# Hybrid decoder trunk: decoding a scan block one step later, right in front of the encoding of the block two further on

## The chip, the core and the metric

The kernel runs on one core of a Trainium2 chip. The core has a matrix engine (TensorE, PE in the rows of the profile, with its weight loads listed apart as PEld), a vector engine (VectorE, DVE), a scalar engine (ScalarE, ACT), a general engine (GpSimd, POOL) and a queue engine that here only issues DMAs (SyncE, SP). The engines run side by side; each takes its own instructions in order and waits on semaphores for the others. The metric is the device time of one launch in microseconds.

## The reference, cut to what matters

A trunk of two layers for 256 positions of width 2048. Layer 0 is a Mamba-2 mixer beside block attention; the change doesn't touch it. Layer 1 is a diagonal complex state-space mixer (S5), and the change lies in its scan.

```
u, gate = split(x @ w_in)                     # 2048 -> 2 x 2048
u_g = u as 128 groups of 16 channels          # each drives 64 complex states
bu  = b_bar[g] @ u_g                          # encode into the states
h_t = lam_bar * h_{t-1} + bu_t                # scan over 256 positions
y   = real(c[g] @ h) + d * u                  # decode
y   = gelu(y)
ga, gb = split(y @ w_glu)
out = (ga * sigmoid(gb) * silu(gate)) @ w_out
x   = layer_norm(alpha * x + out)
```

## The kernel before, in words

**Weights.** All five weight matrices are streamed from memory as 432 chunks of 256 x 512 numbers, here called units. `split_to` loads a unit (SP, L222) and splits it into a high part (ACT, L225) and a low part (DVE, L227), because a product is built from three products of parts. It is called three units ahead of the unit that PE is at; four buffers hold units. PE multiplies a unit in `wmm` (L288, 24 rows of 128x256 in the profile's count) or in `xmm` (L271, 12 rows of 128x512).

**Jobs and steps.** All other work is emitted between the units by `pump`: first the jobs that must be done within the current product (`jobs`), then those that are spread evenly up to a goal (`back`). The scan of layer 1 is such a list. It is made of 16 blocks of 8 groups; `ssm(b)` enters the parts of block b under step numbers, with `at(t, f)`, and each step that is not empty becomes one entry of `back`. The entries are spread over 66 units, beginning at the second product of layer 1. With t = 2b the parts are:

- `load` at t-2: POOL issues the DMA of the block's tables (`wt`, four buffers, L1114)
- `table` at t-1: POOL writes the scan's factors (`rt`, L1121 and L1122)
- `enc` at t: 16 small matmuls on quarters of the array (64x64), from `wt` and the inputs `um` into the PSUM tile `enc` (one buffer, L1131; the profile counts 32 passes)
- `rec1` at t+1: DVE turns the states by their phases (L1141 to L1149)
- `rec2` at t+2: DVE scans and turns back (L1156 to L1159), result `gt` (two buffers)
- `dec` at t+3: 24 small matmuls of the same shape, from `um` (L1172) and `gt` (L1176), into the PSUM tile `dec` (one buffer; the profile counts 48 passes)
- `act` at t+4: ACT applies gelu from PSUM (L1182); after every second block POOL stores the result to memory (L1187, L1188)

After every fourth block the stored result is loaded back in another layout (`y_load`, POOL, L1201) and split into a high and a low part (`y_split`, ACT L1209 and DVE L1210). The product with `w_glu` reads these: `product_pair` runs twelve units on the results of the first twelve blocks and then four units on those of the last four.

**Order.** Within a step the parts stand in the order in which the blocks entered them. A build-time scheduler of the framework then sets the order of each engine's instructions from the order of emission, the dependences and its own estimate of times; it may put large matmuls between small ones. Semaphores come from the dependences. During the steps, jobs of the products stand on ACT too, among them the Silu of the gate half (L1225), which needs another function table than gelu.

Of the kernel before, what the change touches and what calls it, by code (L numbers as in the profile page):

```python
# [159 lines left out]
def trunk(tc, io, out):  # L160
# [8 lines left out]
    with ExitStack() as top:  # L169
# [23 lines left out]
        def big(tag, shape, dt=F32):  # L193
            return slot.tile(shape, dt, tag=tag, name=nm(tag))
# [877 lines left out]
        with ExitStack() as l1:  # L1072
# [3 lines left out]
            def w1(tag, shape, bufs=2, dt=F32):  # L1076
                return wk.tile(shape, dt, tag=tag, bufs=bufs, name=nm(tag))
# [13 lines left out]
            def u_load(hh):  # L1091
                j, h = hh // 2, hh % 2
                u = um[hh] = w1("um", [P, 12, 64], 3)
                for i in range(2):
                    src = ud[j][16 * h + 8 * i : 16 * h + 8 * i + 8].rearrange("q a c -> a q c")
                    at = 64 * (1 - i)
                    nc.gpsimd.dma_start(u[64 * i : 64 * i + 64, 0:8, :], src)
                    nc.gpsimd.dma_start(u[at : at + 64, 8:12, :], src[:, 1::2, :])
# [3 lines left out]
            def at(t, f):  # L1102
                steps.setdefault(t, []).append(f)
# [3 lines left out]
            def ssm(b):  # L1107
# [80 lines left out]
                            nc.gpsimd.dma_start(dst[1, :, 1 - i], ys[64:128, i])  # L1188

                t = 2 * b  # L1190
                at(t + 4, act)
                at(t + 3, dec)
                at(t + 2, rec2)
                at(t + 1, rec1)
                at(t, enc)
# [3 lines left out]
            def y_load(j):  # L1199
                y5[j] = w1("ut", [P, 4, S], 1)  # L1200
                nc.gpsimd.dma_start(y5[j], yd[j].rearrange("g a c -> (g a c)").rearrange("(f p t) -> p f t", p=P, t=S))  # L1201

            def y_split(j):
                if j == 0:
                    y5["h"] = big("A", [P, KT, S], F32R)
                    y5["l"] = big("B", [P, KT, S], F32R)
                yt = y5[j]
                fs = slice(4 * j, 4 * j + 4)
                A.activation(y5["h"][:, fs, :], yt, AF.Copy)  # L1209
                V.tensor_tensor(y5["l"][:, fs, :], yt, y5["h"][:, fs, :].bitcast(F32), op=OP.subtract)  # L1210

            for b in range(16):
                ssm(b)
                if b % 2 == 0:
                    at(2 * b - 2, lambda b=b: u_load(b // 2))
                if b % 4 == 3:
                    at(2 * b + 6, lambda b=b: y_load(b // 4))
                    at(2 * b + 9, lambda b=b: y_split(b // 4))
            sg1 = wk.tile([P, 2, D], F32, tag="sg1", bufs=1, name="sg1")
            for j in range(8):  # L1220
                ps = product("w" if j < 4 else "x", x1hl) if j else first1
# [105 lines left out]
```

## Time and profile before

| | us |
|---|---|
| median of 3 runs | 1364.88 |
| lowest, highest | 1363.3, 1366.78 |
| profiled execution | 1366.41 |
| its span, first to last instruction | 1364.6 |
| busy: PE / PEld / DVE / ACT / POOL | 1349.1 / 1214.1 / 982.8 / 673.3 / 372.3 |
| first encode to last decode | 915.5 to 1100.2 |

The times of the table's first three rows are of whole launches; the span is that of the instructions in the profiled one. In a row of the profile stand the engine, the line of the kernel, the operation, the tiles written and read, and the shape. PE's matmuls overlap in the array, so that the durations of rows in a sequence add up to more than the time they take; the time from one start to the next is what counts. "Idle before" is only a cost on an engine that bounds the stage.

### The profile page before, as it was taken

What the parts mean: (1) busy time and instruction counts of PE and PEld (TensorE: products, weight loads), DVE (VectorE), ACT (ScalarE), POOL (GpSimd) and SP (SyncE); (2) the same over time, 40 slices, a digit from 0 to 9 for tenths busy, and PEclk for the clock granted to TensorE, in tenths of its full rate; (3) what the DMA queues carried; (4) which work ended last, traced back from release to release, by engine and by line L of the source; (5) the groups of instructions that cost most, each with busy time, mean ns of one, the idle gap of its engine ahead of it and who ended that gap; (6) DMA issues with size and microseconds to landing.
All of it is one profiled execution on the core that took longest, in us unless ns stands there. A gap on an engine that the chain in (4) does not pass through costs nothing.

```text
span 1364.6 us, 25068 instructions
## 1 busy us (share of the span) xinstructions
PE 1349.1 (99%) x9918; PEld 1214.1 (89%) x9918; DVE 982.8 (72%) x1559; ACT 673.3 (49%) x869; POOL 372.3 (27%) x649
## 2 busy tenths in 40 slices
PE   9999999999999999999999999999999999999996
PEld 9999999998998998998988888899977788888885
DVE  5789746687688779689788766748788856555555
ACT  5565557764543543554554344344344545444441
POOL 0140000123027628616788700013243100000001
PEclk9999999999999999999999999899999999999998
DMA  8556555545546756756767779397888666666762
GB/s 308 173 156 201 176 169 166 155 140 170 184 125 208 254 164 205 261 169 207 256 203 229 216 231 315 121 303 247 288 269 300 210 211 191 187 189 187 256 215 78
DMA packets 80742, 283.02 MB, mean 207 GB/s; under 512 B 9840, under 2 KB 12528, under 8 KB 80112
## 3 DMA queue, kind: packets, MB, share of 16 engines
q1 hardware_dynamic: 68112, 239.33, 55.5%
q0 software_dynamic: 7328, 30.42, 6.8%
q10 hardware_dynamic: 5184, 11.67, 2.2%
q8 instruction: 78, 1.28, 0.4%
q14 instruction: 40, 0.33, 0.1%
HBM read 260.41 MB, written 20.97 MB: 206 GB/s over the span
## 4 chain that ended last, share of the span: by engine, by line
PE 94%; DVE 4%; DMA 1%; issue 1%; ACT 0%; POOL 0%; POOLq 0%; DVEq 0%
PE main L288 43%; PE main L271 43%; DVE wl L227 1%; PE aux L358 1%; PE enc L1131 1%; PE aux L794 1%; PE dec L1176 1%; PE aux L701 1%; PE aux L367 1%; DMA bc<-in_s5bc 1%; PE aux L906 1%; PE aux L874 1%; PE aux L764 0%; PE dec L1172 0%; PE aux L697 0%
## 5 line engine op out<-in xcount | busy, mean ns | idle before, releaser
L227 DVE TENSOR_TENSOR wl<-raw,wh 128x1024 fp32r<-128x1024 f32 x431 | 538.5, 1251 | 329.5 <-ACT wh L225 323.4
L225 ACT ACTIVATE wh<-raw 128x1024 fp32r<-128x1024 f32 x431 | 456.1, 1059 | 579.1 <-PE main L271 266.0
L288 PE MATMUL main<-A,wh 128*128 128x256 f32 x1408 | 402.6, 286 | 0.0
L288 PE MATMUL main<-B,wh 128*128 128x256 f32 x1408 | 400.1, 284 | 0.0
L288 PE MATMUL main<-A,wl 128*128 128x256 f32 x1408 | 399.9, 284 | 0.0
L288 PEld LDWEIGHTS main<-A,wh 128*128 128x128 f32 x1408 | 270.8, 192 | 0.6 <-issue 0.2
L288 PEld LDWEIGHTS main<-B,wh 128*128 128x128 f32 x1408 | 270.8, 192 | 0.4
L288 PEld LDWEIGHTS main<-A,wl 128*128 128x128 f32 x1408 | 270.7, 192 | 0.2 <-issue 0.2
L271 PE MATMUL main<-wl,A 128*128 128x512 f32 x512 | 200.4, 391 | 0.5 <-DVE wl L227 0.3
L271 PE MATMUL main<-wh,A 128*128 128x512 f32 x512 | 200.4, 392 | 0.0
L271 PE MATMUL main<-wh,B 128*128 128x512 f32 x512 | 200.0, 391 | 0.0
L271 PE MATMUL main<-wh,C 128*128 128x512 f32 x384 | 152.0, 397 | 0.0
L271 PE MATMUL main<-wh,F 128*128 128x512 f32 x384 | 150.0, 391 | 0.0
L271 PE MATMUL main<-wl,C 128*128 128x512 f32 x384 | 149.8, 390 | 0.0
L635 POOL TENSOR_TENSOR c<-c 128x8 f32<-128x8 f32 (+2 forms) x192 | 108.0, 581 | 28.8 <-DMA wb<-c 21.3
L271 PEld LDWEIGHTS main<-wl,A 128*128 128x128 f32 x512 | 96.2, 188 | 20.9 <-DVE wl L227 1.3
L271 PEld LDWEIGHTS main<-wh,B 128*128 128x128 f32 x512 | 96.2, 188 | 19.9
L271 PEld LDWEIGHTS main<-wh,A 128*128 128x128 f32 x512 | 96.2, 188 | 19.8 <-issue 0.2
L271 PEld LDWEIGHTS main<-wh,C 128*128 128x128 f32 x384 | 72.1, 188 | 15.5
L271 PEld LDWEIGHTS main<-wh,F 128*128 128x128 f32 x384 | 72.1, 188 | 15.4
L271 PEld LDWEIGHTS main<-wl,C 128*128 128x128 f32 x384 | 72.1, 188 | 14.3
L804 POOL TENSOR_TENSOR ssq<-ssq,c 128x256 f32<-128x256 f32 x16 | 17.6, 1099 | 210.2 <-ACT c L802 209.6
(279 smaller groups left out, 1680.6 us busy)
## 6 DMA issues: line engine op xcount, KB each, us to landing
raw<-in_wi SPq DMA_DIRECT2D x271, 512.0 KB, 4.0
raw<-in_wo SPq DMA_DIRECT2D x96, 512.0 KB, 4.3
raw<-in_wglu SPq DMA_DIRECT2D x64, 512.0 KB, 3.7
wt<-wb POOLq DMA_DIRECT2D x16, 896.0 KB, 7.6
wb<-ob ACTq DMA_DIRECT2D x16, 512.0 KB, 5.5
bc<-in_s5bc SPq DMA_DIRECT2D x16, 256.0 KB, 4.4
wb<-c POOLq DMA_DIRECT2D x16, 256.0 KB, 4.1
wb<-om ACTq DMA_DIRECT2D x16, 128.0 KB, 4.1
```

What stands on the lines that cost most here:

```text
L225: high = A.activation(wh, raw, AF.Copy)
L227: splits[n] = (high, V.tensor_tensor(wl, raw, wh.bitcast(F32), op=OP.subtract))
L271: T.matmul(ps[o], l[:, k, sl], r[:, j, :], start=start and i == 0, stop=stop and i == 2)
L288: T.matmul(pv[o // 2][:, o % 2, :], l[:, j, sl], r[:, k, :], start=first and i == 0 and o % 2 == 0, stop=end and i == 2 and o % 2 == 1, sk ...
L358: end = T.transpose(dst[:, i * P : i * P + P], s, ident)
L367: T.matmul(px[:64, 0:64], idle, idle, start=i == 0, stop=i == n - 1)
L635: G.tensor_tensor(p[:, :, :, 0:m], cs[:, :, :, 1 : m + 1], cs[:, i, :, n : n + 1].unsqueeze(1).to_broadcast([P, 2, 4, m]), op=OP.mult)
L701: T.matmul(pk[at : at + 64, a * 16 : a * 16 + 16], ev[:, a, 64 * i : 64 * i + 64], cv[:, a, i, :], start=True, stop=True)
L794: T.matmul(yo, xs[:, 0, xc], df[:, i, 0:256], start=True, stop=False)
L804: G.tensor_tensor(ssq, ssq, jk[:, f, :], op=OP.add)
L874: T.matmul(px[:, 128:384], qT[:, h, P:S], kT[:, h, :], start=True, stop=True)
L906: T.matmul(po, v[:, 0, hs], pT[:, i, 0:256], start=True, stop=False)
```

## The change

The decode of a block moves from step 2b+3 to step 2b+4, and gelu from 2b+4 to 2b+5. Step 2b+4 is the one in which block b+2 is encoded, and as block b entered its parts first, its decode stands directly in front of that encode. The load back and the split of the finished results move by one step as well. Nothing else is changed: no instruction is added or taken out.

```
                 t = 2 * b
-                at(t + 4, act)
-                at(t + 3, dec)
+                at(t + 5, act)
+                at(t + 4, dec)
                 at(t + 2, rec2)
                 at(t + 1, rec1)
                 at(t, enc)
...
                 if b % 4 == 3:
-                    at(2 * b + 6, lambda b=b: y_load(b // 4))
-                    at(2 * b + 9, lambda b=b: y_split(b // 4))
+                    at(2 * b + 7, lambda b=b: y_load(b // 4))
+                    at(2 * b + 10, lambda b=b: y_split(b // 4))
```

## The prediction

> **What bounds the kernel now.** I read the page first, then the list of waits of PE, then the sums of each engine over the scan stage, then PE's rows one by one.
>
> ```profile
> span 1364.6 us, 25068 instructions
> ...
> PE 94%; DVE 4%; DMA 1%; issue 1%; ACT 0%; POOL 0%; POOLq 0%; DVEq 0%
> ...
> PE aux L358 <- DVE D L1016: 1.4, 2, 1.3
> PE aux L367 <- POOL idle L362: 0.9, 1, 0.9
> PE main L288 <- DVE F L1030: 0.9, 1, 0.9
> PE main L288 <- ACT C L1026: 0.6, 2, 0.3
> PE main L271 <- DVE wl L227: 0.3, 1, 0.3
> ...
> 905.00:1101.00 196.00, 196.00 (x2248) 166.72 (x2247) 157.21 (x222) 89.32 (x101) 60.23 (x107) 1.00 0.81 259
> ```
>
> The chain that ends last is PE for 94% of the span. The five rows after it are all the waits of PE in the whole run, 4.1 us together, and no encode (L1131) or decode (L1172, L1176) is among them. The last row is the scan stage (columns: PE, PE weight loads, DVE, ACT, POOL, clock, DMA share, GB/s): PE is busy in all 196.0 us at the full clock, DVE in 157.2, ACT in 89.3, POOL in 60.2. So what PE does here is paid one for one, and what the other engines do is free as long as it isn't late.
>
> PE's rows around one whole decode and one whole encode (start, duration, instruction):
>
> ```profile
> 998.16 0.39 PE L271 MATMUL main<-wh,F 128*128 128x512 f32 x1
> 998.48 0.34 PE L1172 MATMUL dec<-um,wt 64*64 64x64 f32 x8
> 998.64 0.41 PE L1176 MATMUL dec<-gt,wt 64*64 64x63 f32 x16
> 998.87 0.30 PE L1172 MATMUL dec<-um,wt 64*64 64x64 f32 x8
> 998.99 0.41 PE L1176 MATMUL dec<-gt,wt 64*64 64x63 f32 x16
> 999.33 0.50 PE L271 MATMUL main<-wh,C 128*128 128x512 f32 x1
> 999.67 0.40 PE L271 MATMUL main<-wl,C 128*128 128x512 f32 x1
> 999.90 0.39 PE L271 MATMUL main<-wh,F 128*128 128x512 f32 x1
> ...
> 925.92 0.28 PE L288 MATMUL main<-C,wl 128*128 128x256 f32 x1
> 926.12 0.69 PE L1131 MATMUL enc<-um,wt 64*64 64x64 f32 x32
> 926.75 0.39 PE L288 MATMUL main<-C,wh 128*128 128x256 f32 x1
> 926.97 0.28 PE L288 MATMUL main<-F,wh 128*128 128x256 f32 x1
> 927.09 0.28 PE L288 MATMUL main<-C,wl 128*128 128x256 f32 x1
> ...
> 929.61 0.28 PE L288 MATMUL main<-C,wl 128*128 128x256 f32 x1
> 929.82 0.34 PE L1172 MATMUL dec<-um,wt 64*64 64x64 f32 x8
> 930.09 0.39 PE L288 MATMUL main<-C,wh 128*128 128x256 f32 x1
> 930.32 0.28 PE L288 MATMUL main<-F,wh 128*128 128x256 f32 x1
> ```
>
> Ends of matmuls are modelled, so I use starts. Undisturbed large matmuls start every 0.23 us (L271) or 0.12 us (L288). From 998.16 to 999.90 lie three large starts, 0.68 us by themselves, in 1.74 us: the decode of 48 passes costs 1.06. From 925.92 to 927.09 the same way: 1.17 - 0.36 = 0.81 for an encode of 32 passes. From 929.61 to 930.32: 0.71 - 0.24 = 0.47 for 8 passes, the first piece of a decode that stands in two pieces. A line through the three gives 0.015 us a pass, which the starts inside the decode confirm (998.87 to 998.99, 0.12 for 8), and a fixed price: 0.47 - 0.12 = 0.35, 0.81 - 0.48 = 0.33, 1.06 - 0.72 = 0.34. Each visit of PE to the 64x64 shape thus costs **0.34 us** whatever it does there. The rows show where: 998.16 to 998.48 is 0.09 longer than 0.23 on the way in; on the way out the first large matmul starts about 0.13 late and the second one (999.33 to 999.67) 0.11.
>
> **The change, part by part.**
>
> *Visits of PE.* In the built order of the kernel before, the 16 encodes make 17 visits (block 0's stands in two) and the 16 decodes 22 (those of blocks 0, 3, 7, 10, 13 and 15 stand in two, with large matmuls between): 39. In the built order of the changed kernel there are two for encode 0, one for encode 1, fourteen in which decode b-2 runs straight into encode b (b from 2 to 15), and decodes 14 and 15 alone, none of them in pieces: 19. Passes and large matmuls are the same in number. 20 visits fewer at 0.336 (the three fits, unrounded) are **-6.7 us**.
>
> *The seam.* No row of before shows a decode followed at once by an encode. Below, it costs nothing: the nearest row is the seam inside the decode, from L1172 to L1176 with other tiles and operands, where the next start comes after 0.12 us for eight passes as it does anywhere else (998.64 to 998.87, from L1176 back to L1172, is 0.23 for 16). Above, it costs a whole visit, 14 x 0.336 = 4.7 us. I take nothing, as the nearest row is of the same shape on the same engine. The Trainium skill (TensorEngine Tiling (Array Packing), Tiling Modes, key properties) states that a change of the tiling mode, and not one of the tile alone, drains TensorE; by it the seam is free as well, which no run here shows yet.
>
> *What the fixed price is.* Should the 0.09 on the way in be the first matmul's semaphore wait rather than the shape, each of the 14 seams keeps it: 14 x 0.09 = 1.3 us, and the sum is -5.4. The Trainium skill (TensorE: Matmul & The Clock Gate, Part 3, The cost: per-tile semaphore tail) speaks against the full gain: it gives a tail of 25 + 4.7 per tile + 26.3 ns per increment where packed tiles end, 70 ns for four tiles and one increment; as an estimate by that, the 14 merged visits keep 14 x 0.07 = 1.0 us and the sum would be -5.7, inside the bounds that the forecast has below without it. The trace speaks for the shape: the piece at 929.82, at whose end no other engine's work is released, pays the same 0.35.
>
> *Steps.* The stage has 40 non-empty steps where it had 39, spread over the same number of weight units: each comes 2.5% closer. Nothing on PE changes by that.
>
> *DVE.* The two reconstruction steps keep their places in the step list; a decode now has two steps instead of one between its input and itself. With 157.2 us of work in a stage that shrinks to 189, DVE is at 83% and hidden.
>
> *ACT, POOL and the DMAs.* Gelu (ACT, 16 x 0.38 us), the four stores after every second block (POOL, 0.62 each), the load back and the split of the result all move one step later, together. Two chains have to be looked at, and the buffers.
>
> ```profile
> 1005.23 1.05 ACT L225 ACTIVATE wh<-raw 128x1024 fp32r<-128x1024 f32 x1
> ...
> 1033.05 1.28 ACT L1225 ACT_TABLE_LOAD   x1
> 1034.35 1.09 ACT L1225 ACTIVATE sg<-main 128x512 f32<-128x512 f32 x2
> ...
> 1036.85 1.28 ACT L1182 ACT_TABLE_LOAD   x1
> 1038.15 0.38 ACT L1182 ACTIVATE ys<-dec 128x256 f32<-128x256 f32 x1
> ...
> 1056.42 0.55 POOL L1114 DMA_DIRECT2D wt<-wb  x1 [5.87 <-PE dec L1176]
> ...
> wt<-wb POOLq DMA_DIRECT2D x12, 896.0 KB, 7.6
> ...
> 1082.34 0.62 PE enc L1131 x32
> ...
> 1100.24 14.98 PE main L271 x65
> ...
> 1100.31 0.38 ACT L1182 ACTIVATE ys<-dec 128x256 f32<-128x256 f32 x1 [1.34 <-PE dec L1176]
> ...
> 1111.72 1.06 ACT L1209 ACTIVATE A<-ut 128x1024 fp32r<-128x1024 f32 x1 [0.40 <-DMA ut<-yd]
> ...
> 1112.82 1.23 DVE L1210 TENSOR_TENSOR B<-ut,A 128x1024 fp32r<-128x1024 f32 x1 [0.23 <-ACT A L1209]
> ```
>
> The table buffers (wt, four): the load for block 15 issues at 1056.42, when decode 11 ends, lands about 7.6 later and is used at 1082.34. One step is half the distance of two encodes, about 5.6 us, so 25.9 - 5.6 - 7.6 = 12.7 us are left. POOL waits longer at that load, and the stores of the blocks stand behind it, but what waits for them in turn is the load back, three steps ahead of its split. Cost nothing; if the cover went, PE would wait at an encode.
>
> The one decode buffer in PSUM: decode b+1 waits for the gelu of block b. In the built order the tightest places are blocks 6 and 11, where gelu stands on ACT behind a weight split, Silu and two table loads: 1.05 + 1.28 + 1.09 + 1.28 + 0.38 = 5.1 us from the end of a unit, while PE has 30 large matmuls, 6.8 us, before the next decode. 1.7 us are left; elsewhere more.
>
> The last block: the result must be split before the second half of the first gated product pair starts, 91 large matmuls after 1100.24, at 1120.9; it ends at 1114.05, 6.9 us early. In the new order decode 15 stands 5 matmuls earlier, but gelu is behind one more weight split (about 2.3 us later) and the split behind one more unit; the 11.0 us from gelu's end to the split's start stay. I get 4.3 us left. Cost nothing.
>
> **Sum.** -6.7 us: the profiled execution, 1366.4 us with a span of 1364.6 (1.8 us lie around it), would come to 1359.7; the median of the three runs, 1364.88, is 1.5 below the profiled one and comes to **1358.2 us**.
>
> **Rivals.**
>
> *The seam costs.* The encode's own waits and the change of PSUM bank take part of a visit. For it: no row shows the seam. Against it: the seams inside a decode are free. At the full price 6 visits are saved, -2.0 us, 1362.9; at the way-in price -5.4, 1359.5.
>
> *The gain is given back to the weight stream.* PE runs each unit sooner, and the loads, at 259 GB/s over the stage, would have to bring 268. For it: DMA engines are 81% busy. Against it: PE doesn't wait for a weight split in this stage once, and each split is placed three units ahead. All of it given back: 1364.9.
>
> *Slower: PE stops at the merged visit for gelu.* The place is the one decode buffer; the encode now stands behind the decode in PE's order, so a late gelu holds both and everything after. It decides from 1.7 us of lateness at blocks 6 and 11, more elsewhere. To end 4.1 us above before it must cost 10.8 us, 0.8 at each of the 13 visits behind the first: 1369. Against it: ACT is busy in 89 of 196 us, and the lateness would have to be more than 2 us at nearly every block.
>
> *The change doesn't do what it says*: excluded by the built order.
>
> **How the numbers follow.** The forecast (gain 5 to 7.5) has 0.78; the seam 0.11, two thirds of it below 4.1 us of gain; given back 0.07; slower by gelu 0.04. 0.3% is 4.1 us, about what a measurement of this kernel can tell from no change; the runs themselves scatter by 1.5 to 2 us around their median. Faster by more than that: 0.78 plus a third of 0.11 and some of the partly given back, 0.83. Within: 0.13. Slower: 0.04. The range goes from 7.0 us of gain (20 x 0.35) and 1.2 of scatter, 1356.7, widened to 1356, up to the way-in price with its scatter and a part of the seam, 1362.
>
> **What would show it.** In the chain of waits of the changed kernel, the encodes and decodes stand together with about 19 visits, the rows of a merged visit last about 0.13 + 80 x 0.015 = 1.33 us from its first start to the next large one, and insert 1.53 with the late second one. The list of PE's waits holds no encode or decode. Scan stage to the last decode: about 6 us shorter; the rest of the run as long as before. Wrong would be: a gap in front of the encode inside a visit (the seam), PE waiting for ACT at L1172 (gelu) or for DVE wl at L271 (the weight stream), or the last split behind the product pair's second half.

## The result, and the profile after

| | before | after |
|---|---|---|
| median of the runs on one chip, us | 1364.53 | 1356.62 |
| lowest, highest | 1363.3, 1366.78 | 1355.84, 1359.39 |
| profiled execution, us | 1366.41 | 1359.26 |
| its span, us | 1364.6 | 1357.5 |

The ratio of the changed kernel to the kernel before is 0.9944, with a 95% interval from 0.9934 to 0.9955: 0.56% faster, 7.6 us by the ratio, 7.9 us by the medians. In a second set of runs it was 0.9942 [0.9929, 0.9956], so a gain well below 1% stands clear of the scatter.

The first lines below are from the changed kernel's page, and the rows with `<-` are all of PE's waits in its whole run (total us, times, longest):

```profile
span 1357.5 us, 25068 instructions
...
PE 94%; DVE 4%; DMA 1%; issue 0%; ACT 0%; POOL 0%; POOLq 0%; ACTq 0%; DVEq 0%
...
PE aux L358 <- DVE D L1016: 1.7, 2, 1.3
PE main L288 <- DVE F L1030: 1.2, 1, 1.2
PE aux L367 <- POOL idle L362: 0.9, 1, 0.9
PE main L271 <- DVE wl L227: 0.6, 2, 0.3
PE main L288 <- ACT C L1026: 0.3, 1, 0.3
```

The shape of the page is that of before: the chain is PE for 94%, and no encode or decode is among the waits.

To compare stages I take the time from the first matmul of the 285th weight unit to that of the 345th, a stretch that holds the whole scan in every kernel here. Summed over just that stretch (columns: PE, PE weight loads, DVE, ACT, POOL, clock, DMA share, GB/s), before:

```profile
910.39:1110.07 199.68, 199.68 (x2242) 168.82 (x2241) 158.44 (x223) 90.67 (x102) 60.18 (x107) 1.00 0.81 256
```

and after:

```profile
910.52:1102.91 192.39, 192.39 (x2242) 167.80 (x2241) 158.22 (x223) 89.61 (x102) 61.40 (x107) 1.00 0.83 265
```

The same 2242 matmuls take **192.39 us in place of 199.68: 7.29 less**. What follows the stretch lasts 254.57 us in both and, to 0.02 us, in every kernel below. What lies ahead of it scatters: in the ten traces with the same number of warm-up matmuls the stretch starts between 907.28 and 910.60 us. Two stretches at half clock, near 869 and 879 us, are there in some executions and not in others (granted clock 0.66 from 868 to 873 us in the profile of after, 1.00 in that of the kernel with the encode first). The profiles of before and after both have them. So I compare the stretch below, and give the whole time's ratio beside it.

A merged visit in the changed kernel (PE's rows: start, duration, instruction):

```profile
988.05 0.39 PE L271 MATMUL main<-wh,C 128*128 128x512 f32 x1
988.27 0.39 PE L271 MATMUL main<-wl,C 128*128 128x512 f32 x1
988.50 0.39 PE L271 MATMUL main<-wh,F 128*128 128x512 f32 x1
988.82 0.34 PE L1172 MATMUL dec<-um,wt 64*64 64x64 f32 x8
988.98 0.41 PE L1176 MATMUL dec<-gt,wt 64*64 64x63 f32 x16
989.22 0.30 PE L1172 MATMUL dec<-um,wt 64*64 64x64 f32 x8
989.33 0.41 PE L1176 MATMUL dec<-gt,wt 64*64 64x63 f32 x16
989.57 0.65 PE L1131 MATMUL enc<-um,wt 64*64 64x64 f32 x32
990.14 0.50 PE L271 MATMUL main<-wh,C 128*128 128x512 f32 x1
990.48 0.39 PE L271 MATMUL main<-wl,C 128*128 128x512 f32 x1
990.71 0.40 PE L271 MATMUL main<-wh,F 128*128 128x512 f32 x1
...
993.00 0.39 PE L271 MATMUL main<-wh,C 128*128 128x512 f32 x1
```

The decode runs into the encode: from the last 16 passes of L1176 to the encode are 0.24 us, and the same 16 passes inside the decode take as long (988.98 to 989.22). From the first small start to the next large one are 1.32 us. The way in is 0.32, 0.09 more than a large matmul needs; the large matmul after the first is again 0.11 late (990.14 to 990.48).

### The profile page after: what moved, and what is told of

It reads as the page before. It is cut to its first block, busy times and chain, and to the rows that moved or that the text cites. A ratio compares the mean times of both kernels' runs of the same rounds, so it can differ in the third digit from the quotient of the medians.

```text
span 1357.5 us, 25068 instructions
## 1 busy us (share of the span) xinstructions
PE 1341.5 (99%) x9918; PEld 1212.9 (89%) x9918; DVE 980.6 (72%) x1559; ACT 671.7 (49%) x869; POOL 367.0 (27%) x649
## 3 DMA queue, kind: packets, MB, share of 16 engines
q8 instruction: 78, 1.28, 0.4%
## 4 chain that ended last, share of the span: by engine, by line
PE 94%; DVE 4%; DMA 1%; issue 0%; ACT 0%; POOL 0%; POOLq 0%; ACTq 0%; DVEq 0%
PE main L288 43%; PE main L271 43%; DVE wl L227 1%; PE aux L358 1%; PE aux L794 1%; PE aux L701 1%; PE enc L1131 1%; PE aux L367 1%; DMA bc<-in_s5bc 1%; PE dec L1176 1%; PE aux L906 1%; PE aux L874 1%; PE aux L764 0%; PE dec L1172 0%; PE aux L697 0%
## 5 line engine op out<-in xcount | busy, mean ns | idle before, releaser
L288 PE MATMUL main<-A,wh 128*128 128x256 f32 x1408 | 403.0, 286 | 0.0
L288 PE MATMUL main<-B,wh 128*128 128x256 f32 x1408 | 400.4, 284 | 0.0
L288 PE MATMUL main<-A,wl 128*128 128x256 f32 x1408 | 400.3, 284 | 0.0
L288 PEld LDWEIGHTS main<-A,wh 128*128 128x128 f32 x1408 | 270.9, 192 | 0.6 <-issue 0.2
L288 PEld LDWEIGHTS main<-B,wh 128*128 128x128 f32 x1408 | 271.0, 192 | 0.4
L288 PEld LDWEIGHTS main<-A,wl 128*128 128x128 f32 x1408 | 270.8, 192 | 0.2 <-issue 0.2
L271 PE MATMUL main<-wl,A 128*128 128x512 f32 x512 | 200.6, 392 | 0.6 <-DVE wl L227 0.6
L271 PE MATMUL main<-wh,A 128*128 128x512 f32 x512 | 200.6, 393 | 0.0
L271 PE MATMUL main<-wh,B 128*128 128x512 f32 x512 | 200.0, 391 | 0.0
L271 PE MATMUL main<-wh,C 128*128 128x512 f32 x384 | 150.8, 394 | 0.0
L271 PE MATMUL main<-wh,F 128*128 128x512 f32 x384 | 149.9, 390 | 0.0
L271 PE MATMUL main<-wl,C 128*128 128x512 f32 x384 | 149.8, 390 | 0.0
L271 PEld LDWEIGHTS main<-wl,A 128*128 128x128 f32 x512 | 96.2, 188 | 21.0 <-DVE wl L227 1.4
L271 PEld LDWEIGHTS main<-wh,A 128*128 128x128 f32 x512 | 96.2, 188 | 19.8 <-issue 0.2
L271 PEld LDWEIGHTS main<-wh,B 128*128 128x128 f32 x512 | 96.2, 188 | 19.8
L635 POOL TENSOR_TENSOR c<-c 128x8 f32<-128x8 f32 (+2 forms) x192 | 100.0, 539 | 24.9 <-DMA wb<-c 17.4
L271 PEld LDWEIGHTS main<-wh,F 128*128 128x128 f32 x384 | 72.1, 188 | 15.2
L271 PEld LDWEIGHTS main<-wh,C 128*128 128x128 f32 x384 | 72.1, 188 | 15.1
L271 PEld LDWEIGHTS main<-wl,C 128*128 128x128 f32 x384 | 72.1, 188 | 14.6
```

Of the source, the lines that this page charges most:

```text
L271: T.matmul(ps[o], l[:, k, sl], r[:, j, :], start=start and i == 0, stop=stop and i == 2)
L288: T.matmul(pv[o // 2][:, o % 2, :], l[:, j, sl], r[:, k, :], start=first and i == 0 and o % 2 == 0, stop=end and i == 2 and o % 2 == 1, sk ...
L635: G.tensor_tensor(p[:, :, :, 0:m], cs[:, :, :, 1 : m + 1], cs[:, i, :, n : n + 1].unsqueeze(1).to_broadcast([P, 2, 4, m]), op=OP.mult)
```

## The experiments

The theory was that PE pays a fixed price for each visit to the small matmuls and that their order and neighbours don't matter. The rivals were: the gain comes from the later decode itself (a wait, a buffer), the seam has a price, or the price isn't that of the shape. All kernels in short:

| kernel | visits | stretch, us | to before | ratio of the whole time [95%] |
|---|---|---|---|---|
| before | 39 | 199.68 | | |
| after | 19 | 192.39 | -7.29 | 0.9944 [0.9934, 0.9955] |
| after, again | 19 | 192.41 | -7.27 | 0.9942 [0.9929, 0.9956] |
| one more step later, decode alone | 33 | 197.39 | -2.29 | 0.9981 [0.9970, 0.9992] |
| encode first | 19 | 192.34 | -7.34 | 0.9953 [0.9940, 0.9966] |
| encode in halves | 34 | 198.03 | -1.65 | 0.9988 [0.9979, 0.9996] |
| 16 small visits added | 35 | 203.25 | +3.57 | 1.0015 [1.0006, 1.0024] |
| 16 full-shape visits added | 35 | 199.97 | +0.29 | 0.9995 [0.9986, 1.0004] |
| blocks in pairs | 11 | 191.08 | -8.60 | 0.9943 [0.9929, 0.9956] |
| pairs, tables earlier | 10 | 194.54 | -5.14 | 0.9954 [0.9942, 0.9966] |
| the last, code moved by 4 KB | 10 | 191.58 | -8.10 | one run, 1356.71 us |
| the same by 8 KB | 10 | 189.13 | -10.55 | one run, 1358.11 us |
| the same by 16 KB | 10 | 192.46 | -7.22 | one run, 1368.75 us |
| by 8 KB, narrow warm-up | 10 | 188.98 | -10.70 | 0.9984 [0.9975, 0.9993] |

In the set of the three single runs the kernel before took 1365.72 us.

### Later, but not merged

The decode one more step later, where no encode is:

```
-                at(t + 5, act)
-                at(t + 4, dec)
+                at(t + 6, act)
+                at(t + 5, dec)
...
-                    at(2 * b + 7, lambda b=b: y_load(b // 4))
-                    at(2 * b + 10, lambda b=b: y_split(b // 4))
+                    at(2 * b + 8, lambda b=b: y_load(b // 4))
+                    at(2 * b + 11, lambda b=b: y_split(b // 4))
```

> The decode moves two steps later than in the kernel before (t+5, gelu t+6, load back and split one more step on), so that it has all the time it wants but stands alone between large matmuls. In the built order 33 visits of PE to the 64x64 shape, none of them a decode in two pieces (before 39, changed kernel 19). Theory of the visits, 0.34 to 0.37 us each: 6 visits fewer than before, -2.0 to -2.2 us (about 1362.4 against a before of 1364.5), and 4.8 to 5.2 us slower than the changed kernel. Rival, that the later place with its time for the input made the gain and not the adjacency: as fast as the changed kernel, -7 to -8 us (1356.6).

Its stretch is 2.29 us shorter than before, for six visits fewer (no decode is in pieces any more): 0.38 each. The delay by itself gives nothing else.

### The encode in front of the decode

```
-                at(t, enc)
+                steps.setdefault(t, []).insert(0, enc)
```

> Same step for both, but the encode of block b+2 is emitted ahead of the decode of block b. 19 visits in the built order, in some of them a few passes of the one stand inside the other. Theory of the visits: as the changed kernel, -6.7 to -8 us against before, since a seam costs nothing in either direction. Rival, that each seam costs the first matmul's wait (0.09 us): a visit with two seams instead of one loses up to 0.09, six such visits, 0.5 us slower than the changed kernel. Rival of the lateness: also as the changed kernel.

The stretch is 192.34 us, the same as after to 0.05. PE's rows of one visit in this kernel:

```profile
985.62 0.69 PE L1131 MATMUL enc<-um,wt 64*64 64x64 f32 x32
986.14 0.30 PE L1172 MATMUL dec<-um,wt 64*64 64x64 f32 x8
986.25 0.41 PE L1176 MATMUL dec<-gt,wt 64*64 64x63 f32 x16
986.49 0.30 PE L1172 MATMUL dec<-um,wt 64*64 64x64 f32 x8
```

32 passes of the encode take 0.52 us to the decode's first start, 0.016 a pass, which leaves nothing for the seam. The seam is free in either order, and that the decode is "in front" is not what counts. Only the four visits in which a few passes of the one stand inside the other are dearer, by 0.04 us each.

### The encode in two halves, half a step apart

```
-                def enc():
-                    px = d["x"] = sp.tile([P, 2, 512], F32, tag="enc", name=nm("enc"))
+                def enc(half=0):
+                    if half == 0:
+                        d["x"] = sp.tile([P, 2, 512], F32, tag="enc", name=nm("enc"))
+                    px = d["x"]
...
-                    for q in range(2):
+                    for q in (half,):
...
                 at(t, enc)
+                at(t + 0.5, lambda: enc(1))
```

> The changed kernel with the encode's second half moved to a step of its own half a step later: the same passes in 34 visits of PE instead of 19. Theory of the visits: 15 more at 0.34 to 0.37, 5.1 to 5.5 us slower than the changed kernel (about 1362), 1.7 to 1.9 faster than before. Rival, that the fixed price belongs to the waits and increments at the start and end of an encode or a decode, not to the shape: the second halves wait for nothing new, so at most 15 x 0.09 = 1.3 us slower than the changed kernel (1358). Rival of the lateness: as the changed kernel.

15 visits more than after cost 5.64 us: 0.376 each. The same work, the same order of the decodes, and nearly all of the gain is gone with the visits.

### Is the price the shape's?

One matmul is added to each block, a step behind its decode, so that it stands alone among large ones. It writes columns that nothing reads. In one kernel it is on a quarter of the array, in the other on the whole array:

```
                 def act():
...
+                    T.matmul(d["y"][0:64, 0, 256:320], d["w"][0:64, 0:64], um[b // 2][0:64, 0, :], start=True, stop=True)
```

```
+                    T.matmul(d["y"][:, 0, 256:320], d["w"][:, 0:128], um[b // 2][:, 0, :], start=True, stop=True)
```

> The changed kernel with one matmul added per block, in the step after the decode, between large matmuls: 64x64, of the block's own tables and inputs, into columns of the decode's PSUM tile that nobody reads. 35 visits instead of 19, 16 of them with 2 passes. Theory, that going to the 64x64 shape and back is what costs: 16 x (0.36 + 0.11) = 7.5 us on the scan stage over the changed kernel. Rival, that a visit costs by the waits and increments of an encode or a decode: the added ones wait for nothing new, so 16 x 0.11 = 1.8, at most 16 x 0.20 = 3.2 with a wait of 0.09 each.

> The same as the added small visits, in the same places and of the same tables and inputs, but with the full 128x128 shape. Theory of the shape: nothing for coming and going, 16 x 0.11 = 1.8 us on the scan stage over the changed kernel. Rival, that any interruption of the large matmuls costs, whatever its shape: the same as the added small visits, 7.5 us.

An added visit with the small shape, and the large matmuls around it:

```profile
993.40 0.39 PE L271 MATMUL main<-wh,F 128*128 128x512 f32 x1
993.72 0.33 PE L1179 MATMUL dec<-um,wt 64*64 64x64 f32 x2
993.97 0.50 PE L271 MATMUL main<-wh,C 128*128 128x512 f32 x1
994.31 0.39 PE L271 MATMUL main<-wl,C 128*128 128x512 f32 x1
```

and one with the whole array:

```profile
995.60 0.39 PE L271 MATMUL main<-wh,F 128*128 128x512 f32 x1
995.83 0.33 PE L1179 MATMUL dec<-um,wt 128*128 128x64 f32 x2
995.96 0.48 PE L271 MATMUL main<-wh,C 128*128 128x512 f32 x1
996.28 0.40 PE L271 MATMUL main<-wl,C 128*128 128x512 f32 x1
```

The two large starts after 993.40 come 0.91 us later, where 0.45 would be undisturbed: 0.46 for the small visit. After 995.60 they come 0.68 later: 0.23. Over all sixteen, an added visit took 0.44 us (among L288) or 0.48 (among L271) in the small shape, and 0.22 or 0.275 on the whole array. The way in (0.32 against 0.23) and the first late large start (0.25 after the small matmul, 0.13 after the other) belong to the shape; the second late start (0.34 and 0.32) comes either way. The two stretches differ by 3.28 us, 0.205 per added visit. **So about 0.21 us of what such a visit costs is the shape's; the rest is paid when a small matmul of the full shape breaks the row of large ones, too.** What that rest consists of was not tested. The Trainium skill (TensorEngine Tiling (Array Packing), Tiling Modes, key properties) has TensorE drain at a change of the tiling mode. The 0.21 and the free seam agree with that; the part that remains without a change of mode is not covered by it.

The sixteen visits in the small shape thus took 7.5 us, as the theory had it, and those in the full shape 4.2 where the theory of the shape had 1.8: that expectation was wrong. The stretches are longer than after's by more, 10.86 and 7.58 us.

Most of the difference is in PE's list of waits. The small one:

```profile
PE dec L1172 <- ACT ys L1183: 2.0, 3, 1.2
```

and the one on the whole array:

```profile
PE dec L1172 <- ACT ys L1183: 2.4, 2, 2.0
```

With the late starts behind them these waits cost about 3.1 us in either kernel. Here gelu has to wait for the added matmul and so comes late for the next decode, which stands in one buffer with it: the prediction's slower rival, with its place, in a kernel where gelu has lost its margin.

### More of the same: blocks in pairs

If visits are what is paid, two blocks can be decoded and two encoded in one. The encodes of both blocks go into one PSUM tile, their decodes into another, with one gelu for the two. The tables are split into three tiles so that the decode's part (`loadd`) comes later. The main lines, against the changed kernel:

```
-                    wt = d["w"] = w1("wt", [P, 1792], 4)
-                    nc.gpsimd.dma_start(wt, wb[b])
+                    wt = d["w"] = w1("we", [P, 512], 4)
+                    nc.gpsimd.dma_start(wt, wb[b][:, 0:512])
...
+                def loadd():
+                    wd = d["wd"] = w1("wd", [P, 768], 3)
+                    nc.gpsimd.dma_start(wd, wb[b][:, 512:1280])
...
-                t = 2 * b
-                at(t + 5, act)
-                at(t + 4, dec)
-                at(t + 2, rec2)
-                at(t + 1, rec1)
+                k = b // 2
+                t = 4 * k
+                td = t + (6 if k == 7 else 8)
+                if b2 == 1:
+                    at(td + 1, act)
+                at(td, dec)
+                at(t + 3 + b2, rec2)
+                at(t + 1 + b2, rec1)
```

> The changed kernel taken on: blocks go in pairs. One PSUM tile holds two encodes, one holds two decodes; both decodes of a pair stand in front of both encodes of the pair two further on; gelu is one instruction for a pair; a block's tables come in two loads instead of one, so that they fit in four and three buffers. 11 visits instead of 19. Theory of the visits: 8 fewer at 0.34 to 0.37, 2.7 to 3.0 us faster than the changed kernel, -10 to -11 against before (about 1353.8). Rival, stalls: PE now waits at a pair's visit for the reconstruction of its second block or for the tables; each late one costs its lateness, and the rows would show PE waiting for DVE or a DMA at an encode or decode. Rival of the lateness: as the changed kernel.

Only 1.31 us less than after, where eight visits fewer at 0.365 would give 2.9. PE's list of waits had two new entries in which it waits for nothing that the profile shows, and I took the encode's tables for late. So they were loaded two steps earlier:

```
-                at(t - 3, load)
+                at(t - 3, loadp)
+                at(t - 5, load)
```

> The block pairs with the encode's tables loaded two steps earlier, ahead of the stores in POOL's queue, and 10 visits in the built order instead of 11. Theory: in the pairs' trace PE stood 0.8 us inside one visit in front of the second encode, whose table load had been issued 10 us before behind the stores and the load back; with the load earlier that is gone, and with one visit less the scan stage is 1.2 to 1.7 us shorter than with the pairs (189.4 to 189.9 us from unit 284 to unit 344), 2.5 to 3 shorter than the changed kernel's. Rival, that the pairs lose by something else: it stays at 191 less one visit, 190.7.

It was worse, and the tables are not it. PE's rows at the two places of this kernel:

```profile
954.83 1.13 PE L1144 MATMUL enc<-um,we 64*64 64x64 f32 x64
957.58 0.39 PE L288 MATMUL main<-C,wh 128*128 128x256 f32 x1 [1.62 <-issue]
...
1017.20 1.11 PE L1144 MATMUL enc<-um,we 64*64 64x64 f32 x60
1020.35 0.48 PE L1144 MATMUL enc<-um,we 64*64 64x64 f32 x4 [2.04 <-issue]
1020.76 0.79 PE L271 MATMUL main<-wh,C 128*128 128x512 f32 x1
1021.36 0.63 PE L271 MATMUL main<-wl,C 128*128 128x512 f32 x1
1021.78 0.63 PE L271 MATMUL main<-wh,F 128*128 128x512 f32 x1
```

PE stops once in the middle of an encode, four passes before its end, and once behind it, in front of a large matmul, and neither instruction waits for a semaphore there. The four passes read the same tables as those ahead of them, so a late table is not the cause. Behind the second stop the clock is halved: the large starts come 0.42 apart, and the granted clock is 0.50 from 1020.4 to 1023.7 us.

### Where PE's code is loaded

What is left is PE's own code. The page of before and of every kernel here has two DMA queues that carry instructions. The larger one, in the changed kernel and then in the one below that is moved by 16 KB, which has 128 matmuls and as many weight loads more:

```profile
q8 instruction: 78, 1.28, 0.4%
...
q8 instruction: 79, 1.29, 0.4%
```

78 loads bring 1.28 MB, 16 KB each. PE has 9918 matmuls and as many weight loads (PE and PEld on the page of after), 19,836 instructions. If the queue is PE's, a load brings about 256 of them, an estimate of 64 bytes each; the one load more for 256 more instructions agrees. A pair's visit is 160 passes, 320 instructions in 2.4 us, more than one load; a merged visit of the changed kernel is 160 in 1.3 us. If PE runs out of code there, the stops must move when the code is moved against the edges of the loads, and come back when it is moved by a whole load. The kernel with pairs and earlier tables got 32, 64 or 128 more of the matmuls that warm PE up at the start (4, 8 and 16 KB of code); nothing else is changed:

```
-WARM0 = 70
+WARM0 = 102        # 134, 198
```

> The pairs with the tables earlier, and 32 more warm-up matmuls at the very start of the kernel; in the scan stage no instruction of PE is changed. Theory of the code loads: PE reads its instructions in blocks of 16 KB, 256 instructions, and a pair's visit uses 320 in 2.4 us, so that it runs dry where a block's edge lies badly; 64 more PE instructions in front of the stage move the edges by a quarter of a block, and the gaps, of 1.6 and 2.0 us inside the visits near 953 and 1016 us, move to other visits or shrink. Rival, a late table load or the DMA traffic: the same two gaps in the same two visits.

> As the one before, with 64 more warm-up matmuls: the edges move by half a block. Theory of the code loads: gaps in other visits again, one to three of them, 1 to 3 us each. Rival: the same two gaps in the same two visits.

> As before, with 128 more warm-up matmuls, 256 instructions: the edges come to lie where they were. Theory of the code loads: the gaps are back in the same two visits as without a shift, about 1.6 and 2.0 us (the second, if the clock falls again, longer). Rival, that any difference between the shifts is chance: nothing says where they come.

Moved by 4 KB, the stop of the third visit shrinks from 1.62 to 0.40 us and comes 32 matmuls earlier in the program, inside the encode; that of the sixth is gone, and PE stops at the seventh and the eighth, for 0.37 and 0.98 us. With the late starts behind them the three cost 0.6, 0.7 and 1.3 us. Moved by 8 KB, PE doesn't stop at all, where stops in other visits were expected, and the stretch is 189.13 us. PE's rows of that kernel at the visit where the unmoved one stopped for 2.04:

```profile
1020.45 0.30 PE L1187 MATMUL dec<-um,wd 64*64 64x64 f32 x8
1020.57 0.41 PE L1191 MATMUL dec<-gt,wd 64*64 64x63 f32 x16
1020.80 1.13 PE L1144 MATMUL enc<-um,we 64*64 64x64 f32 x64
1021.86 0.50 PE L271 MATMUL main<-wh,C 128*128 128x512 f32 x1
1022.19 0.40 PE L271 MATMUL main<-wl,C 128*128 128x512 f32 x1
```

Moved by 16 KB, the stops are back at the same two visits, the third and the sixth, and one of them again four passes before the end of the encode:

```profile
967.23 1.13 PE L1144 MATMUL enc<-um,we 64*64 64x64 f32 x64
970.15 0.39 PE L288 MATMUL main<-C,wh 128*128 128x256 f32 x1 [1.80 <-issue]
...
1029.77 1.12 PE L1144 MATMUL enc<-um,we 64*64 64x64 f32 x60
1032.25 0.33 PE L1144 MATMUL enc<-um,we 64*64 64x64 f32 x4 [1.36 <-issue]
```

The period of one load speaks for the code, and the traces show two things more. Counted from the kernel's first matmul, all nine stops (two in each kernel with pairs that isn't moved, three with 4 KB, two with 16 KB) come after a number of matmuls that leaves 64 to 70 on division by 128, so they stand whole loads of 256 instructions apart. And at each of them a load of q8 had started 0.2 to 2.1 us before the stop, and PE went on 1.30 to 1.58 us after it had landed: at the stop of 2.04 us the load runs from 1018.07 to 1019.04, and PE goes on at 1020.35. So PE stops for its code.

An edge between two loads inside a visit is not enough, as a visit of 160 passes is longer than the 128 of a load and always holds one. By the same count every stop stands at the second edge behind the start of its visit, when PE has run through a whole load of small matmuls (for one stop the last eight of the load are large): 128 passes at 0.015 us are 1.9 us, while a load takes about 1.0 us and PE goes on 1.3 us later at the earliest (an estimate from these rows). Moved by 8 KB, no visit holds two edges. Two visits with edges at the passes 6 and 134 went through without a stop, so two are needed but don't always suffice.

Without stops, nine visits fewer than after save 3.26 us, 0.362 each: the fixed price holds down to ten visits.

### A faster kernel?

The kernel moved by 8 KB is not faster than the changed kernel as a whole, since 64 more warm-up matmuls delay the first large one by 6.8 us. The last run made all of them half as wide:

```
-WARM0 = 70
+WARM0 = 134
...
-                T.matmul(px[:64, 0:64], idle, idle, start=i == 0, stop=i == n - 1)
+                T.matmul(px[:64, 0:w], idle, idle[:, 0:w], start=i == 0, stop=i == n - 1)
...
-            warm(WARM0)
+            warm(WARM0, 32)
```

> The blocks in pairs with 64 more warm-up matmuls (128 more PE instructions, 8 KB of its code), as in the run with that shift, but all 134 of them half as wide, so that the warm-up should not grow. Theory (PE runs dry where the edge of a code block falls inside a long visit, and this shift puts no edge there): scan stage 189.1 us again, 10.5 under before and 3.3 under the changed kernel; whole time 1364.5 - 10.5 = 1354.0, ratio to before 0.9923. Rival (the short stage of the run with the shift was luck of one execution): stage 191 to 195, ratio 0.994 to 0.996. If a narrow warm-up matmul takes as long as a wide one, about 5 us are added ahead of the stage and the stage alone decides.

The stretch was 188.98 us, so the short stretch was no luck. (That this shift puts no edge into a long visit is too strong: it leaves no visit with two.) But the whole took 1362.72 us (1360.5 to 1363.91), ratio 0.9984 [0.9975, 0.9993]. PE's first row:

```profile
0.94 14.48 PE L367 MATMUL aux<-idle 128*64 128x32 f32 x134 [0.94 <-POOL idle L362]
```

The wide ones took 14.50 us for 134: at the start a matmul of half the width takes as long, and the code has to be moved in another way. That was not tried. No kernel measured in several runs beats the changed one by more than its interval.

## Why the prediction was right, and where its sizes were off

**The bound: right.** PE is busy in all of the stretch in both kernels, with 2242 matmuls in each, and what it was spared was the gain.

**The visits: right, the price a little low.** 39 became 19, as counted. The prediction's price was 0.336 us; the stretch gives 7.29 / 20 = 0.365. The term that was mis-sized is the way out: the fits ended at the second late large matmul, and two of the three were taken among L288, where the price is lower. The rows of after show that the large ones behind it are late too: from 990.48 to 993.00 lie eleven starts, 2.52 us, where 11 x 0.2266 is 2.49. That is 0.03 per visit among L271, where after's merged visits have a fixed price of 0.36 to 0.40; among L288 it is 0.32 to 0.35. With 0.365 the sum would have been -7.3. By the medians the gain was 7.9 us, a little beyond the 5 to 7.5 of the forecast.

**The seam: right.** Nothing, in either order. The bound above of 0.34 for each, and that rival, fall.

**What the price is: wrong in part.** The prediction put all of it down to the shape. The added visits show about 0.21 for the shape, and a rest that a full-shape matmul between the large ones pays as well. For this change both go together, so it didn't touch the sum. The way-in price of 0.09 is the shape's, as the prediction said: the added matmul on the whole array doesn't pay it. The prediction's estimate of a 70 ns tail by the Trainium skill (TensorE: Matmul & The Clock Gate, Part 3, The cost: per-tile semaphore tail), which a merged visit would have kept, has nothing for it in the trace: the rows above insert 1.53 us (988.50 to 990.71 less three times 0.227), just the forecast without it.

**The hidden engines: right, with less left than worked out.** The gelus of blocks 6 and 11 end 1.5 us ahead of the next decode (predicted 1.7). The last split ends at 1110.4; by before's distance from the stretch's end, the second half of the product pair starts at 1113.7, so 3.3 us are left (predicted 4.3). From gelu's end to the split's start are 11.8 us, where 11.0 was assumed; and the prediction's terms as written, 6.9 and five matmuls (1.1) less 2.3, give 5.7; what takes that to 4.3 it doesn't say. The weight stream brings 265 GB/s (predicted 268) and PE waits for a weight split 0.6 us in the whole run. Given back was nothing. The slower rival needed a gelu later by more than its margin; the kernels with the added matmul made it so, and PE then stopped at L1172 for 2.0 us in three places and 2.4 in two.

**The sum.** Predicted 1359.7 for the profiled execution, measured 1359.26; predicted 1358.2 as the median, measured 1356.62. 0.6 us of the 1.6 come from the visits' price, 0.35 from the median of before in the joint runs (1364.53), and the rest is within the scatter ahead of the stretch.

## What to carry to other kernels

Where TensorE bounds a stage that mixes large matmuls with packed small ones, count the visits to the small ones and not only their passes: beside 0.015 us a pass each visit costs about 0.37 us here, whatever is done in it, and putting two together costs nothing at the seam. Before work is moved, look up the margin of every wait that the moved work sets, such as gelu's 1.5 us here, since the same edit with a little less margin stops TensorE. A visit may also become too long: in the 320 short instructions of a pair's visit TensorE ran out of code, in the 160 of a merged visit it didn't. A stop that the profile gives to "issue", that ends behind an instruction load and moves with the code, is the sign of it.

## What was not expected of the hardware

- PE runs dry of instructions in or just behind the 2.4 us of a pair's visit, for 0.4 to 2.0 us at a time, depending on where the 16 KB loads of its code have their edges; two kernels that differ by 64 matmuls at the very start differ by 3.3 us (189.13 and 192.46) a millisecond later.
- After the stop of 2.04 us the clock was halved for 3.4 us; after those of 1.80 and 1.36 it was not. The Trainium skill (TensorE: Matmul & The Clock Gate, Part 1) has the clock halved after an idle window of about 3.4 us; here the stop was shorter. Near 869 us, in the traces that have the halved clock there, PE's longest wait ahead of it is 1.3 us.
- A quarter of the array isn't the whole price: a full-shape matmul of this kind still costs 0.22 to 0.275 us among the large ones, of which its own passes took 0.13 (995.83 to 995.96).
